# A hybrid transformer block on one core: weights laid out by the host, low halves by accumulating DMA, the residual stream in DRAM, and separate leads for loads and casts

## The chip, the core and the metric

The kernel runs on one core of a Trainium2 chip. The core has a matrix engine (TensorE, PE in the profile, with its weight loads as PEld), three engines for elementwise work (VectorE or DVE, ScalarE or ACT, GpSimd or POOL), and a queue engine (SyncE or SP) that here only issues DMA transfers. Each engine takes its instructions in the order in which the program lists them. The engines share an on-chip memory of 128 partitions (SBUF); matmuls write into eight banks of PSUM. Inputs, weights and the output lie in DRAM.

The metric is the device time of one execution in microseconds (us), lower is better.

## The reference

One layer: an input projection feeds an attention head group and a convolution group, an output projection joins them, and a gated feed-forward network (FFN) follows. Only the last two matter here.

```python
xn = rms_norm(h, norm1_g)
proj = einsum('bsd,dn->bsn', xn, w_in)            # 2048 -> 5120
...                                               # attention and causal convolution
mixed = concatenate([att, u], axis=-1)
h = h + einsum('bsm,md->bsd', mixed, w_out)       # 2048 -> 2048
hn = rms_norm(h, norm2_g)
a  = einsum('bsd,df->bsf', hn, w_gate)            # 2048 -> 5632
bu = einsum('bsd,df->bsf', hn, w_up)              # 2048 -> 5632
h = h + einsum('bsf,fd->bsd', silu(a) * bu, w_down)
```

The sequence has 256 positions, in float32. All weights together are about 200 MB and are read once.

## The kernel before

**Split operands.** PE multiplies operands of a shorter format (fp32r). To keep float32 accuracy every operand is split into a high part (its rounding) and a low part (the rest), and a product is the sum of three matmuls: high × high, high × low, low × high. A weight tile is therefore loaded (`raw`, line 305, by SP), rounded by ACT (`whi`, line 310), and its rest computed by VectorE (`wlo`, line 319: raw − whi). A second way makes the rest without VectorE: ACT writes −whi into `wlo` (line 313), and a POOL DMA adds `raw` to it (line 314). This is "by DMA". The name `by_dma` on a chunk selects it.

**Chunks.** All matrix products form one list of chunks, which `run_chunks` emits in order. A plain chunk is 2 × 128 rows of a weight by 512 columns: 512 KB, 12 matmuls of 512 columns. Chunk t + 2 is loaded and cast ahead of chunk t's multiplication (`AHEAD`); in the fast blocks below loads and roundings run three chunks ahead and subtractions two (`HI_AHEAD`, `LO_AHEAD`). Loads have four `raw` buffers, and every third chunk outside the fast blocks takes a buffer of another pool. `whi` and `wlo` have three each. When a block of columns is complete, a generator (`glu_done`, `out_done`, `block_done`, `down_done`, ...) finishes it, and `resume()` runs the generators step by step between the matmuls.

**Stages.** w_in goes first, in column blocks; then w_out, whose block ends (`out_done`) add the product to the residual stream `h`, kept in SBUF as two tiles of 128 × 2048; then the FFN. Its hidden width of 5632 is eleven blocks of 512 columns, in groups of 4, 4 and 3 (`FGROUPS`). A group computes gate and up for its blocks, transposes the activations, and multiplies them with its rows of w_down; `down_done` adds the result to `h`, and in the last group writes `h` out.

**Fast blocks.** Block 0 uses plain chunks. Blocks 1 to 10 are fast: half of the inner dimension goes through a scheme of seven products for eight. An "s" unit loads two tiles each of w_up and w_gate (`wb`, line 872, two DMAs), forms sums of them on VectorE (`wt`, lines 882 to 884), rounds 7 × 512 columns on ACT (`wh`, lines 885 and 886) and subtracts on VectorE (`wl`, lines 890 and 891); PE then runs 21 matmuls (lines 907 to 909). The other half goes as "g" and "u" units, plain residues of gate and up: a chunk of two tiles, 12 matmuls (lines 924 to 930). A block has four s, four g and four u units in the order of the string `ORDER` (`FIRST` for block 1). The last g and the last u unit of blocks 2 to 10 are by DMA.

At a block's end `products_done` and `block_done` combine eight PSUM sums on VectorE and ACT. `transposed` then turns the activations around on PE (line 801, `ps_a`), in two steps, during the first s unit of the next block; each step's result is split by ACT (`ahi`, line 803) and VectorE (`alo`, line 805).

**Order.** Nothing is scheduled by a machine: each engine's order is the order in which the Python code emits. An instruction that waits holds up all that stand behind it on its engine.

## Time and profile before

| what | value |
|---|---|
| time, median of 3 runs | 1081.56 us (1081.28 to 1082.33) |
| the profiled execution's span | 1078.5 us, granted clock 0.995 |
| matmul instructions of PE | 4834 |
| weights and inputs read | 200.04 MB |
| w_in, w_out | about 6 to 255, 255 to 345 us |
| FFN block 0 | 345 to 397 us |
| fast blocks 1 to 3, their w_down | 397 to 531, 531 to 619 us |
| fast blocks 4 to 7, their w_down | 619 to 789, 789 to 877 us |
| fast blocks 8 to 10, their w_down | 877 to 1004, 1004 to 1074 us |

The profile is of one execution, and its span leaves out what lies around it in the measured time. A row of the timeline gives start and duration in us, the engine, the source line, the operation, what it writes and reads by the program's names (buffer numbers left out), and in brackets how long the engine was idle just before and on which instruction that ended. A matmul's duration is longer than the distance to the next one, since matmuls are pipelined; the distance between starts is the pace.

### The profile page before, as it was taken

Reading aid. Unit: us, or ns where it says so; the run is one execution under the profiler, and the core shown is the slowest. Engines: PE = TensorE matmul, PEld = TensorE weight load, DVE = VectorE, ACT = ScalarE, POOL = GpSimd, SP = SyncE. Lnnn points to the kernel's source line nnn. Section 1 sums busy time; section 2 is a strip of 40 time slices with the busy share of each in tenths; the row PEclk is TensorE's granted clock in tenths of the full one; section 3 lists DMA queues with packets and bytes.
Section 4 is the critical chain, followed back from the end, with each engine's and each line's share of the span. In section 5 each row is a group of like instructions: output and inputs, shape, how many; then the busy total and the mean of one; then the engine's idle time right before and its main releaser. Section 6 shows DMA issues by size and latency. Waiting matters only on the chain.

```text
span 1078.5 us, 13236 instructions
## 1 busy us (share of the span) xinstructions
PE 1054.6 (98%) x4834; PEld 871.6 (81%) x4834; DVE 844.6 (78%) x1025; ACT 587.1 (54%) x765; POOL 62.8 (6%) x101
## 2 busy tenths in 40 slices
PE   8999999999999999899999999999999999999998
PEld 7888888877888887788888888878788888887786
DVE  4799989898765689988754699889865589898553
ACT  6544567755765655555443456655643355555332
POOL 0030021200100000000000000000000000000000
PEclk9999999999999999999999999999999999999999
DMA  8856665554446575576565777767566668666661
GB/s 243 257 178 199 190 185 169 155 173 157 137 156 195 161 248 197 195 215 194 176 215 183 243 248 212 212 214 230 163 201 221 201 215 263 208 207 176 215 210 63
DMA packets 120941, 212.45 MB, mean 197 GB/s; under 512 B 7220, under 2 KB 29166, under 8 KB 120876
## 3 DMA queue, kind: packets, MB, share of 16 engines
q1 hardware_dynamic: 117744, 200.56, 58.2%
q0 software_dynamic: 3072, 11.01, 4.9%
q8 instruction: 38, 0.62, 0.3%
q14 instruction: 27, 0.22, 0.1%
q10 hardware_dynamic: 60, 0.03, 0.0%
HBM read 200.04 MB, written 2.10 MB: 187 GB/s over the span
## 4 chain that ended last, share of the span: by engine, by line
PE 70%; DVE 15%; issue 6%; ACT 5%; DMA 2%; POOL 1%; SPq 0%; DVEq 0%; ACTq 0%
PE acc L355 16%; PE acc L350 16%; PE acc L349 16%; DVE wlo L319 4%; PE q L924 3%; PE q L925 3%; PE q L930 3%; PE q L907 3%; PE q L908 3%; PE q L909 3%; ACT wh L886 3%; DVE wt L882 2%; DVE wt L883 1%; DVE wt L884 1%; DVE y L488 1%
## 5 line engine op out<-in xcount | busy, mean ns | idle before, releaser
L319 DVE TENSOR_TENSOR wlo<-raw,whi 128x1024 fp32r<-128x1024 f32 (+1 forms) x279 | 337.6, 1218 | 136.8 <-ACT whi L310 136.8
L310 ACT CAST whi<-raw 128x1024 fp32r<-128x1024 f32 (+1 forms) x297 | 309.5, 1049 | 226.9 <-PE acc L350 167.0
L350 PE MATMUL acc<-whi,alo 128*128 128x512 f32 x384 | 150.6, 392 | 2.3 <-DVE alo L805 2.3
L349 PE MATMUL acc<-whi,ahi 128*128 128x512 f32 x384 | 150.4, 392 | 0.0
L886 ACT CAST wh<-wt 128x2048 fp32r<-128x2048 f32 x40 | 76.6, 1914 | 128.8 <-DVE wt L884 128.8
L349 PE MATMUL acc<-whi,xhi 128*128 128x512 f32 (+1 forms) x352 | 129.9, 375 | 4.0 <-ACT xhi L224 2.5
L350 PE MATMUL acc<-whi,xlo 128*128 128x512 f32 (+1 forms) x352 | 128.3, 371 | 0.5 <-DVE xlo L225 0.4
L924 PE MATMUL q<-whi,chi 128*128 128x512 f32 x320 | 124.7, 390 | 0.0
L925 PE MATMUL q<-whi,clo 128*128 128x512 f32 x320 | 124.6, 389 | 0.0
L907 PE MATMUL q<-wh,fhi 128*128 128x512 f32 x280 | 111.1, 397 | 2.1 <-DVE alo L805 2.1
L909 PE MATMUL q<-wl,fhi 128*128 128x512 f32 x280 | 110.4, 394 | 2.3 <-DVE wl L891 2.3
L908 PE MATMUL q<-wh,flo 128*128 128x512 f32 x280 | 110.2, 393 | 0.0
L488 DVE SCALAR_TENSOR_TENSOR y<-upad,cw,y 128x256 f32<-128x256 f32 x240 | 103.3, 480 | 2.1 <-ACT y L481 1.6
L355 PE MATMUL acc<-wlo,ahi 128*128 128x512 f32 x384 | 103.7, 391 | 0.0
L891 DVE TENSOR_TENSOR wl<-wt,wh 128x2048 fp32r<-128x2048 f32 x40 | 91.6, 2290 | 9.4 <-ACT wh L886 9.4
L355 PE MATMUL acc<-wlo,xhi 128*128 128x512 f32 (+1 forms) x352 | 88.2, 375 | 1.1 <-DVE wlo L319 1.1
L350 PEld LDWEIGHTS acc<-whi,alo 128*128 128x128 f32 x384 | 72.6, 189 | 17.8 <-DVE alo L805 2.6
L930 PE MATMUL q<-wlo,chi 128*128 128x512 f32 x320 | 86.4, 392 | 0.0
L349 PEld LDWEIGHTS acc<-whi,ahi 128*128 128x128 f32 x384 | 72.5, 189 | 15.3 <-ACT ahi L803 0.2
L355 PEld LDWEIGHTS acc<-wlo,ahi 128*128 128x128 f32 x384 | 71.8, 189 | 14.6
L349 PEld LDWEIGHTS acc<-whi,xhi 128*128 128x128 f32 x352 | 66.3, 188 | 15.9 <-ACT xhi L224 2.9
L350 PEld LDWEIGHTS acc<-whi,xlo 128*128 128x128 f32 x352 | 66.3, 188 | 11.9 <-DVE xlo L225 0.9
(194 smaller groups left out, 1413.5 us busy)
## 6 DMA issues: line engine op xcount, KB each, us to landing
raw<-in_w_down_dram SPq DMA_DIRECT2D x88, 512.0 KB, 4.0
raw<-in_w_in_dram SPq DMA_DIRECT2D x48, 512.0 KB, 3.8
raw<-in_w_gate_dram SPq DMA_DIRECT2D x48, 512.0 KB, 4.6
raw<-in_w_up_dram SPq DMA_DIRECT2D x48, 512.0 KB, 3.8
wb<-in_w_up_dram SPq DMA_DIRECT2D x40, 512.0 KB, 4.4
wb<-in_w_gate_dram SPq DMA_DIRECT2D x40, 512.0 KB, 5.7
raw<-in_w_out_dram SPq DMA_DIRECT2D x32, 512.0 KB, 3.6
raw<-in_w_in_dram SPq DMA_DIRECT2D x62, 256.0 KB, 3.7
```

The costliest lines, as they stand in the source:

```text
L310: act.copy(c["hi"], c["raw"])
L319: dve.tensor_tensor(c["lo"], c["raw"], c["hi"].bitcast(F32), ALU.subtract)
L349: pe.matmul(ps[m], xhi[:, ms], hi[:, j, :], start=c["first"] and j == 0, stop=False)
L350: pe.matmul(ps[m], xlo[:, ms], hi[:, j, :], start=False, stop=False)
L355: pe.matmul(ps[m], xhi[:, ms], lo[:, j, :], start=False, stop=c["last"] and j == nk - 1)
L488: dve.scalar_tensor_tensor(y[:, ct, :], src, wk, y[:, ct, :], ALU.mult, ALU.add)
L907: pe.matmul(ps, fhi[:, f, p, :], c["hi"][:, w], start=bool(first), stop=False)
L908: pe.matmul(ps, flo[:, f, p, :], c["hi"][:, w], start=False, stop=False)
L909: pe.matmul(ps, fhi[:, f, p, :], c["lo"][:, w], start=False, stop=bool(last))
L924: pe.matmul(ps, x1[:, ms], hi[:, i, :], start=i == 0 and bool(c["first"].get(q)), stop=False)
L925: pe.matmul(ps, x2[:, ms], hi[:, i, :], start=False, stop=False)
L930: pe.matmul(sum_bank(c, q), forms["plain"][k][0][:, ms], lo[:, i, :], start=False, stop=i == 1 and bool(c["last"].get(q)))
```

## The change

- **Host-laid weights.** All weights come as one flat array, in which every chunk's bytes stand in the order in which its tile holds them. `weights()` records the pieces while the program is written, and the host fills the array. A chunk is one DMA with 4 KB per partition where before it was pieces of 512 B to 2 KB and, for the paired columns of the convolution blocks, two DMAs; an s unit is one DMA of 1 MB where before it was two.
- **By DMA.** Which units are by DMA is now written in capitals in `ORDER` and `FIRST`: two of four g and three of four u units in blocks 2 to 10 (five of eight; before two of eight), and three in block 1 (before none).
- **h in DRAM.** `out_done` also writes `h` to the output array, by POOL DMAs. The tiles of `h` lie in a pool that ends with the FFN's beginning. In groups 0 and 1 `down_done` no longer adds on VectorE: ACT copies the PSUM sum (`part`), and a POOL DMA adds it into the output array. In the last group SP fetches the array's content (`so_far`, `fetch_sums`), VectorE adds to it, and it is written out as before.
- **Leads and buffers.** In the fast blocks loads run five chunks ahead, ACT's roundings for by-DMA units five, other roundings three, subtractions two. `raw` gets five buffers, `whi` and `wlo` four.

VectorE at the boundary of the fast blocks 5 and 6: the end of one block's sums (lines 987 and 989; 1013 and 1015 in the changed code), then the first s unit of the next and the first `alo`. Before:

```order
L987 TENSOR_TENSOR sum_6121<-q_5870,sum_6121 128x512
L987 TENSOR_TENSOR sum_6123<-q_6042,sum_6123 128x512
L989 TENSOR_TENSOR sum_6121<-sum_6121,sum_6120 128x512
L989 TENSOR_TENSOR sum_6123<-sum_6123,sum_6122 128x512
L319 TENSOR_TENSOR wlo<-raw,whi 128x1024
L882 TENSOR_TENSOR wt<-wb 128x1024
L883 TENSOR_TENSOR wt<-wb,wt 128x512
L884 TENSOR_TENSOR wt<-wt,wb 128x512
L890 TENSOR_TENSOR wl<-wb,wh 128x1536
L891 TENSOR_TENSOR wl<-wt,wh 128x2048
L319 TENSOR_TENSOR wlo<-raw,whi 128x1024
L805 TENSOR_TENSOR alo_6220<-ps_a,ahi_6219 128x512
```

and after:

```order
L1013 TENSOR_TENSOR sum_6115<-q_5865,sum_6115 128x512
L1013 TENSOR_TENSOR sum_6117<-q_6035,sum_6117 128x512
L1015 TENSOR_TENSOR sum_6115<-sum_6115,sum_6114 128x512
L1015 TENSOR_TENSOR sum_6117<-sum_6117,sum_6116 128x512
L907 TENSOR_TENSOR wt<-wb 128x1024
L908 TENSOR_TENSOR wt<-wb,wt 128x512
L909 TENSOR_TENSOR wt<-wt,wb 128x512
L915 TENSOR_TENSOR wl<-wb,wh 128x1536
L916 TENSOR_TENSOR wl<-wt,wh 128x2048
L326 TENSOR_TENSOR wlo<-raw,whi 128x1024
L831 TENSOR_TENSOR alo_6214<-ps_a,ahi_6213 128x512
```

The `wlo` subtraction between the sums and the s unit's `wt` is gone; the one ahead of `alo` stays. (In the changed code the lines stand lower: 310, 313 and 319 are 317, 320 and 326; 803 and 805 are 829 and 831; 882 to 891 are 907 to 916.)

ACT at the same place, from a `wh` to the second `ahi` of the boundary. Before:

```order
L886 CAST wh<-wt 128x2048
L310 CAST whi<-raw 128x1024
L803 CAST ahi_6219<-ps_a 128x512
L310 CAST whi<-raw 128x1024
L313 ACTIVATE wlo<-raw 128x1024
L885 CAST wh<-wb 128x1536
L886 CAST wh<-wt 128x2048
L803 CAST ahi_6269<-ps_a 128x512
```

and after:

```order
L910 CAST wh<-wb 128x1536
L911 CAST wh<-wt 128x2048
L317 CAST whi<-raw 128x1024
L829 CAST ahi_6213<-ps_a 128x512
L317 CAST whi<-raw 128x1024
L320 ACTIVATE wlo<-raw 128x1024
L317 CAST whi<-raw 128x1024
L320 ACTIVATE wlo<-raw 128x1024
L910 CAST wh<-wb 128x1536
L911 CAST wh<-wt 128x2048
L829 CAST ahi_6267<-ps_a 128x512
```

Between the two `ahi` stand two pairs of a rounding and a negated copy where before there was one.

SP at the last w_down, which begins with the w_down rows (`raw`) behind the last unit of block 10. Before:

```order
L872 DMA wb<-in_w_up_dram 128x2x512
L872 DMA wb<-in_w_gate_dram 128x2x512
L305 DMA raw<-in_w_up_dram 128x2x512 x2
L305 DMA raw<-in_w_down_dram 128x2x512 x24
L1004 DMA out_dram<-h_81 128x256 x2
L1004 DMA out_dram<-h_82 128x256 x2
```

and after:

```order
L898 DMA wb<-in_wts_dram 128x2048
L313 DMA raw<-in_wts_dram 128x1024 x9
L1025 DMA so_far<-out_dram 128x512 x2
L313 DMA raw<-in_wts_dram 128x1024 x2
L1025 DMA so_far<-out_dram 128x512 x2
L313 DMA raw<-in_wts_dram 128x1024 x6
L1025 DMA so_far<-out_dram 128x512 x2
L313 DMA raw<-in_wts_dram 128x1024 x6
L1025 DMA so_far<-out_dram 128x512 x2
L313 DMA raw<-in_wts_dram 128x1024 x3
L1044 DMA out_dram<-so_far 128x256 x4
```

The sums' fetches stand among the weight loads now, the first of them behind the loads of the last u units and seven chunks of w_down.

The diff, its core:

```diff
 AHEAD = 2
-RAW_BUFS = 4
+RAW_BUFS = 5
...
 LAG = (3, 2, 6)
-HL_BUFS = 3
+HL_BUFS = 4
...
 TWOS = [tuple(REST[i : i + 2]) for i in range(0, len(REST), 2)]
-BY_DMA = TWOS[-1:]
-
-ORDER = "sggsggsuusuu"
-
-FIRST = "gugusgsusgsu"
+
+ORDER = "sgGsgGsUUsUu"
+
+FIRST = "gugusgsUsGsU"
...
 PRODUCTS = ((Q1, 0, 5), (Q6, 5, 1), (Q7, 6, 2), (Q5, 4, 3), (Q2, 1, 6), (Q4, 3, 0), (Q3, 2, 4))
-HI_AHEAD, LO_AHEAD = 3, 2
+LOAD_AHEAD, DMA_AHEAD, HI_AHEAD, LO_AHEAD = 5, 5, 3, 2
...
     aux_ps = ctx.enter_context(tc.tile_pool(name="aux", bufs=AUX, space=PSUM))
-    h = [const.tile([P, D], F32, tag=f"h{m}", name=f"h{m}") for m in range(NM)]
+    h = [pre.tile([P, D], F32, tag=f"h{m}", name=f"h{m}", bufs=1) for m in range(NM)]
...
                                done=done if i == len(ks) else None, spare=spare, by_dma=False,
-                               rows=slice(part[0], part[-1] + 1), load=load_chunk, round=round_chunk,
+                               load=load_chunk, round=round_chunk,
                                split=split_chunk, multiply=multiply))
+
+    next_weight = [0]
+
+    def weights(parts):
+
+        n = sum(w for _, _, _, w in parts)
+        src = wts[next_weight[0] : next_weight[0] + P * n].rearrange("(p n) -> p n", n=n)
+        placed_at.append((next_weight[0], n, parts))
+        next_weight[0] += P * n
+        return src
...
             c["raw"] = view(wp.tile([P, NK * N], F32, tag="raw", name="raw", bufs=RAW_BUFS))
-        o = 0
-        rows = c["w"].rearrange("(k p) n -> p k n", p=P)
-        for col, n in c["cols"]:
-            sp.dma_start(out=c["raw"][:, :, o : o + n], in_=rows[:, c["rows"], col : col + n])
-            o += n
+        ks = c["ks"] if "ks" in c else range(c["k0"], c["k0"] + c["nk"])
+        src = weights([(c["w"], k, col, n) for k in ks for col, n in c["cols"]])
+        sp.dma_start(out=c["raw"].rearrange("p k n -> p (k n)"), in_=src)
...
         n = len(chunks)
-        i = j = 0
+        loaded = split = 0
+        rounded = [0, 0]
+
+        def load(i):
+            if i in before:
+                before[i]()
+            chunks[i]["load"](chunks[i])
+
+        def do_round(which, until):
+            while rounded[which] < min(n, until):
+                c = chunks[rounded[which]]
+                if c["by_dma"] == bool(which):
+                    c["round"](c)
+                rounded[which] += 1
+
         for t in range(n):
-            hi_lead, lo_lead = lead(t)
-            while j < min(i, t + 1 + lo_lead):
-                chunks[j]["split"](chunks[j])
-                j += 1
-            while i < min(n, t + 1 + hi_lead):
-                if i in before:
-                    before[i]()
-                chunks[i]["load"](chunks[i])
-                chunks[i]["round"](chunks[i])
-                i += 1
-                if hi_lead == lo_lead:
-                    chunks[j]["split"](chunks[j])
-                    j += 1
-            while j < min(n, t + 1 + lo_lead):
-                chunks[j]["split"](chunks[j])
-                j += 1
+            load_lead, dma_lead, hi_lead, lo_lead = lead(t)
+            while split < min(rounded[0], t + 1 + lo_lead):
+                chunks[split]["split"](chunks[split])
+                split += 1
+            while loaded < min(n, t + 1 + load_lead):
+                load(loaded)
+                loaded += 1
+                if load_lead == lo_lead:
+                    do_round(1, loaded)
+                    do_round(0, loaded)
+                    chunks[split]["split"](chunks[split])
+                    split += 1
+            do_round(1, t + 1 + dma_lead)
+            do_round(0, t + 1 + hi_lead)
+            while split < min(n, t + 1 + lo_lead):
+                chunks[split]["split"](chunks[split])
+                split += 1
+            if t in fetch_at:
+                fetch_sums(fetch_at[t])
...
             dve.tensor_tensor(h[m][:, cs], h[m][:, cs], ps[m], ALU.add)
+        for m in range(NM):
+            pool.dma_start(out=out[m * P : (m + 1) * P, cs], in_=h[m][:, cs])
...
         c["b"] = early.tile([P, 4, N], F32, tag="wb", name="wb")
-        for i, w in enumerate((w_up, w_gate)):
-            sp.dma_start(out=c["b"][:, 2 * i : 2 * i + 2, :],
-                         in_=w.rearrange("(k p) n -> p k n", p=P)[:, c["k"] :: HK, c["col"] : c["col"] + N])
+        src = weights([(w, k, c["col"], N) for w in ("w_up", "w_gate") for k in (c["k"], c["k"] + HK)])
+        sp.dma_start(out=c["b"].rearrange("p k n -> p (k n)"), in_=src)
...
         left = dict(s=list(range(NS)), g=list(TWOS), u=list(TWOS))
-        for kind in order:
+        for unit in order:
+            kind = unit.lower()
...
             if kind == "s":
-                c.update(k=what, col=j * N, load=load_pair, round=round_pair, split=split_pair,
+                c.update(k=what, col=j * N, by_dma=False, load=load_pair, round=round_pair, split=split_pair,
...
             else:
-                c.update(ks=what, w=w_gate if kind == "g" else w_up, nk=2, width=N, cols=[(j * N, N)],
-                         rows=slice(what[0], what[1] + 1, what[1] - what[0]), by_dma=j > 1 and what in BY_DMA,
+                c.update(ks=what, w="w_gate" if kind == "g" else "w_up", nk=2, width=N, cols=[(j * N, N)],
+                         by_dma=unit.isupper(),
...
         yield from transposed(j, u)
+    so_far, fetch_at = {}, {}
+
+    def fetch_sums(n):
+        so_far[n] = []
+        for m in range(NM):
+            t = ffn["pool"].tile([P, N], F32, tag=f"sum{n % 2 * NM + m}", name="so_far")
+            sp.dma_start(out=t, in_=out[m * P : (m + 1) * P, n * N : (n + 1) * N])
+            so_far[n].append(t)
+
...
         cs = slice(n * N, (n + 1) * N)
-        parts = 2 if g == len(FGROUPS) - 1 and n == D // N - 1 else 1
-        for m in range(NM):
+        if g < len(FGROUPS) - 1:
+            for m in range(NM):
+                t = ffn["pool"].tile([P, N], F32, tag=f"sum{n % 2 * NM + m}", name="part")
+                act.copy(t, ps[m])
+                pool.dma_start(out=out[m * P : (m + 1) * P, cs], in_=t, accum_op=ALU.add)
+            return
+        parts = 2 if n == D // N - 1 else 1
+        for m in range(NM):
+            t = so_far[n][m]
...
                 hs = slice(cs.start + i * w, cs.start + (i + 1) * w)
-                dve.tensor_tensor(h[m][:, hs], h[m][:, hs], ps[m][:, ws], ALU.add)
-                if g == len(FGROUPS) - 1:
-
-                    (sp if n == D // N - 1 else pool).dma_start(out=out[m * P : (m + 1) * P, hs], in_=h[m][:, hs])
+                dve.tensor_tensor(t[:, ws], t[:, ws], ps[m][:, ws], ALU.add)
+                (sp if n == D // N - 1 else pool).dma_start(out=out[m * P : (m + 1) * P, hs], in_=t[:, ws])
...
             at = len(chunks)
-            block(w_down, n * N, range(j0 * 4, (j0 + nb) * 4), fa, lambda ps, g=g, n=n: down_done(g, n, ps))
+            if g == len(FGROUPS) - 1:
+                fetch_at[at + (0 if n else FGROUPS[g] * N // P // NK - 2)] = n
+            block("w_down", n * N, range(j0 * 4, (j0 + nb) * 4), fa, lambda ps, g=g, n=n: down_done(g, n, ps))
...
         j0 += nb
-    lead = lambda t: (1, 1) if t < len(XPARTS) else (HI_AHEAD, LO_AHEAD) if "kind" in chunks[t] else (AHEAD, AHEAD)
+    lead = lambda t: ((1,) * 4 if t < len(XPARTS) else (LOAD_AHEAD, DMA_AHEAD, HI_AHEAD, LO_AHEAD)
+                      if "kind" in chunks[t] else (AHEAD,) * 4)
...
     run_chunks()
-_FLAT = {"x": (S, D), "w_in": (D, 5120), "conv_w": (1, W, 1, CC), "w_out": (D, D), "w_gate": (D, FF),
-         "w_up": (D, FF), "w_down": (FF, D)}
+_FLAT = {"x": (S, D), "conv_w": (1, W, 1, CC)}
+_WEIGHTS = {"w_in": (D, 5120), "w_out": (D, D), "w_gate": (D, FF), "w_up": (D, FF), "w_down": (FF, D)}
...
     given["rope"] = rope_constants()
+    total = sum(a * b for a, b in _WEIGHTS.values())
+    flat = np.empty(total, np.float32)
+    given["wts"] = flat
...
     args.append(nc.dram_tensor("out_0_dram", (S, D), F32, kind="ExternalOutput").ap())
+    placed_at = []
     with tile.TileContext(nc) as tc, tc.manual_schedule():
-        tile_block(tc, *args)
+        tile_block(tc, *args, placed_at)
+    ws = {name: np.asarray(inputs[name], dtype=np.float32).reshape(shape) for name, shape in _WEIGHTS.items()}
+    assert sum(P * n for _, n, _ in placed_at) == total
+    for o, n, parts in placed_at:
+        tiles = [ws[w][k * P : (k + 1) * P, col : col + c] for w, k, col, c in parts]
+        flat[o : o + P * n] = np.concatenate(tiles, axis=1).ravel()
```

More of the change, by code (lines that the diff above doesn't have):

```diff
@@ L104, in tile_block @@
     tc: tile.TileContext,
-    x, w_in, conv_w, w_out, w_gate, w_up, w_down, gains, vecs, rope, out,
+    x, conv_w, gains, vecs, rope, wts, out, placed_at,
 ):
@@ L1012, in tile_block @@
     for nct in CONV_BLOCKS:
-        block(w_in, [(GC + c0 * P, nct * P), (AC + c0 * P, nct * P)], range(KD), fx,
+        block("w_in", [(GC + c0 * P, nct * P), (AC + c0 * P, nct * P)], range(KD), fx,
               lambda ps, c0=c0, nct=nct: glu_done(c0, nct, ps), cuts=[len(p) for p in XPARTS] if c0 == 0 else ())
@@ L1016, in tile_block @@
     for b in range(2):
-        block(w_in, KC + b * N, range(KD), fx, lambda ps, b=b: qk_done("k", b, ps))
-        block(w_in, QC + b * N, range(KD), fx, lambda ps, b=b: qk_done("q", b, ps))
+        block("w_in", KC + b * N, range(KD), fx, lambda ps, b=b: qk_done("k", b, ps))
+        block("w_in", QC + b * N, range(KD), fx, lambda ps, b=b: qk_done("q", b, ps))
     for b in range(2):
-        block(w_in, VC + b * N, range(KD), fx, lambda ps, b=b: v_done(b, ps))
+        block("w_in", VC + b * N, range(KD), fx, lambda ps, b=b: v_done(b, ps))
     for ks, first, last in ((range(0, 4), True, False), (range(4, 8), False, False), (range(8, 16), False, True)):
         for n in range(3):
-            block(w_out, n * N, ks, fm, (lambda ps, n=n: out_done(n, ps)) if last else None,
+            block("w_out", n * N, ks, fm, (lambda ps, n=n: out_done(n, ps)) if last else None,
                   bkey=("o", n), first=first, last=last, spare=n == 2)
-    block(w_out, 3 * N, range(16), fm, lambda ps: out_done(3, ps))
+    block("w_out", 3 * N, range(16), fm, lambda ps: out_done(3, ps))
     for i, c in enumerate(chunks[len(XPARTS) : -12]):
```

4 lines of the change are left out of this document (2 added, 2 removed).

## The prediction

> **What bounds the kernel now.** I read the page first, then the clock by core, the table by stage, TensorE's waits, and the timelines around the longest of them.
>
> ```profile
> PE 1054.6 (98%) x4834; PEld 871.6 (81%) x4834; DVE 844.6 (78%) x1025; ACT 587.1 (54%) x765; POOL 62.8 (6%) x101
> core 0: 1078.5 us, clock 0.995
> 397.00:455.00 58.00, 55.59 (x242) 44.85 (x240) 55.66 (x53) 31.05 (x27) 0.00 (x0) 0.97 0.62 211
> 455.00:498.00 43.00, 40.59 (x175) 33.40 (x176) 39.24 (x39) 24.85 (x23) 1.99 (x2) 0.96 0.73 219
> 667.00:711.00 44.00, 44.00 (x201) 36.37 (x200) 40.23 (x39) 25.77 (x24) 1.77 (x2) 1.00 0.72 215
> 1004.00:1030.00 26.00, 23.69 (x102) 19.14 (x101) 17.43 (x21) 9.81 (x12) 1.14 (x2) 0.93 0.51 172
> PE ps_a L801 <- DVE alo L805: 5.1, 5, 1.2
> ```
>
> The window rows give start and end, length, busy time of PE, PEld, DVE, ACT and POOL, the granted clock, the DMA share and GB/s. PE is busy 98% of the span and the change leaves its list of matmuls as it is, so only PE's stalls can be won. The windows are the first fast gate-and-up block (397), the second (455), a later one (667) and the start of the last w_down (1004). VectorE works 55.66 of 58 us in the first and 40.23 of 44 us in the later one: there it is all but full, and PE's stalls follow it. Start, duration and instruction are the columns below:
>
> ```profile
> 410.32 0.39 PE L909 MATMUL q<-wl,fhi 128*128 128x512 f32 x1
> 412.82 0.50 PE L907 MATMUL q<-wh,fhi 128*128 128x512 f32 x1 [2.11 <-DVE alo L805]
> ...
> 414.45 0.63 PE L909 MATMUL q<-wl,fhi 128*128 128x512 f32 x1
> 414.88 0.63 PE L907 MATMUL q<-wh,fhi 128*128 128x512 f32 x1
> ...
> 454.30 0.40 PE L908 MATMUL q<-wh,flo 128*128 128x512 f32 x1
> 456.18 0.50 PE L909 MATMUL q<-wl,fhi 128*128 128x512 f32 x1 [1.48 <-DVE wl L891]
> 457.92 1.05 PE L801 MATMUL ps_a<-ident,sum 128*128 128x128 f32 x4 [1.23 <-DVE alo L805]
> ...
> 713.40 0.39 PE L907 MATMUL q<-wh,fhi 128*128 128x512 f32 x1
> 713.63 0.39 PE L908 MATMUL q<-wh,flo 128*128 128x512 f32 x1
> 714.30 0.51 PE L909 MATMUL q<-wl,fhi 128*128 128x512 f32 x1 [0.29 <-DVE wl L891]
> 716.04 0.66 PE L801 MATMUL ps_a<-ident,sum 128*128 128x128 f32 x4 [1.23 <-DVE alo L805]
> 757.42 0.39 PE L908 MATMUL q<-wh,flo 128*128 128x512 f32 x1
> ...
> 1018.52 0.40 PE L349 MATMUL acc<-whi,ahi 128*128 128x512 f32 x1
> 1021.23 0.80 PE L350 MATMUL acc<-whi,alo 128*128 128x512 f32 x1 [2.31 <-DVE alo L805]
> ```
>
> Undisturbed matmuls follow each other at 713.63 − 713.40 = 0.23 us (0.227 over longer runs). What a stall costs is the step between starts less that pace:
> - First and second fast block: 412.82 − 410.32 − 0.23 = 2.27; 457.92 − 454.30 − 0.46 = 3.16. After both, the pace falls to 414.88 − 414.45 = 0.43. The clock columns price this: 0.03 × 58 + 0.04 × 43 = 3.4 us. Sum C = 8.8.
> - Later boundaries: 716.04 − 713.63 − 0.45 = 1.96. Of the five waits of transposes for `alo` (5.1 us), four like the two shown make 4.9, so the fifth is 0.2; one of the four is that at 457.92, which leaves three boundaries of this kind. Sum D = 5.9.
> - Start of the last w_down: 1021.23 − 1018.52 − 0.23 = 2.48, and 0.07 × 26 = 1.8 of clock. Sum E = 4.3.
>
> **Accumulating DMAs for VectorE's subtractions.** The same boundary on VectorE, the last one's two rows, and the costs by group:
>
> ```profile
> 706.18 1.22 DVE L319 TENSOR_TENSOR wlo<-raw,whi 128x1024 fp32r<-128x1024 f32 x1
> ...
> 711.96 2.29 DVE L891 TENSOR_TENSOR wl<-wt,wh 128x2048 fp32r<-128x2048 f32 x1 [0.31 <-ACT wh L886]
> 714.17 1.22 DVE L319 TENSOR_TENSOR wlo<-raw,whi 128x1024 fp32r<-128x1024 f32 x1
> 715.30 0.68 DVE L805 TENSOR_TENSOR alo<-ps_a,ahi 128x512 fp32r<-128x512 f32 x1
> ...
> 715.16 1.46 ACT L885 CAST wh<-wb 128x1536 fp32r<-128x1536 f32 x1
> 718.61 1.91 ACT L886 CAST wh<-wt 128x2048 fp32r<-128x2048 f32 x1 [1.99 <-DVE wt L884]
> ...
> 1018.27 1.05 ACT L310 CAST whi<-raw 128x1024 fp32r<-128x1024 f32 x1
> 1019.35 1.23 DVE L319 TENSOR_TENSOR wlo<-raw,whi 128x1024 fp32r<-128x1024 f32 x1 [2.41 <-ACT whi L310]
> ...
> L313 ACT ACTIVATE wlo<-raw 128x1024 fp32r<-128x1024 f32 x18 | 19.1, 1059 | 0.0
> L314 POOL DMA_DIRECT2D wlo<-raw x18 | 16.1, 894 | 613.8 <-DVE wlo L319 227.5 <-DVE wl L891 215.4 <-ACT wlo L313 134.2
> q1 hardware_dynamic: 117744, 200.56, 58.2%
> q0 software_dynamic: 3072, 11.01, 4.9%
> wlo<-raw POOLq DMA_DIRECT2D x18, 512.0 KB, 6.9
> ```
>
> By-DMA residues go from 18 to 48: two to five in nine blocks, none to three in the first fast block. VectorE loses 30 subtractions of 1.22 us: 3.66 of its 40.23 us in a later block. One of them, at 706.18, stood ahead of the s unit's whole chain (wt, wh on ACT, wl), two more earlier in the block. The late wl (0.29) needs 0.5 us and the late `alo` 1.5 us, so 3.66 us of room covers both unless ACT ends later. D falls by 5.4, between 0 (ACT decides instead) and 5.9.
>
> ACT gains 30 negated copies of 1.06 us, three in a block: 25.77 + 3.2 = 29 us of 42, not full. But they come five units ahead, so the second `ahi` of a boundary stands behind whi, wlo, whi, wlo, wh, wh rather than whi, wlo, wh, wh. From the end of the first `ahi` that is 2 × (1.05 + 1.06) + 1.46 + 1.91 = 7.6 us, where before it was 5.5 and a wait of 1.99 for VectorE: 0.1 later, if the wait goes. Two of a block's casts must also wait until PE frees one of the four whi buffers, and hold up what ACT has behind them. I put +1 in all, from 0 to +4.5 (0.5 us at nine boundaries, a quarter of one cast pair's 2.1).
>
> POOL issues three more DMAs a block, 0.89 us each, with a median landing 6.9 us later; the residue is used five units of 2.7 to 4.8 us after its cast, at least 13 us. Nothing waits there, by this estimate.
>
> In the first fast block three subtractions go, and the loads' lead of five replaces what this row shows just ahead of it:
>
> ```profile
> 394.81 1.05 ACT L310 CAST whi<-raw 128x1024 fp32r<-128x1024 f32 x1 [3.55 <-DMA raw<-in_w_up_dram]
> ```
>
> ACT was idle 3.55 us for a load, and VectorE behind it. I leave 0.9 of the stall of 2.27 and 0.3 of the second one, and take the slow pace after both as gone: C falls by 7.6, between 4.7 (half of the stalls and of the slow pace stay) and 8.5.
>
> **The last w_down.** `alo` stood behind a `wlo` that waited 2.41 us for a cast issued behind `ahi` on ACT. The changed order puts that cast ahead of `ahi`; only the 0.68 us `alo` remains, and 0.3 of E stays: −4.0, between 0 and −4.3.
>
> **h in DRAM.** Sixteen additions leave VectorE; sixteen ACT copies and accumulating DMAs replace them in the w_down of groups 0 and 1, where PE does not stall for ACT now: nothing, and the cover is the two chunks of 2.7 us each that stand ready while ACT copies. The eight writes of h lie beside the last w_out. In the last w_down SP fetches the sums; the first fetch waits on SP for the output's last accumulation and holds back weight loads behind it. I put +0.5, between 0 and +2.7 (one chunk of 12 matmuls at 0.227).
>
> **Weights laid out by the host.** Same bytes, one DMA for two in the first columns.
>
> ```profile
> PE acc L349 <- ACT xhi L224: 2.5, 2, 1.5
> PE acc L349 <- ACT whi L310: 1.5, 2, 0.8
> raw<-in_w_in_dram SPq DMA_DIRECT2D x48, 512.0 KB, 3.8
> raw<-in_w_in_dram SPq DMA_DIRECT2D x62, 256.0 KB, 3.7
> 3.61 0.95 SPq L305 DMA_DIRECT2D raw<-in_w_in_dram  x2
> ```
>
> A pair cost SP 0.95 us, one costs half; three pairs stand ahead of the fourth x load. PE waited 4.0 us in all at the start. I take half, −2; between 0 and −4. Later on I cost the layout at nothing, since the lead hides a landing: of one matrix, 256 KB took 3.7 us to land and 512 KB 3.8, so longer transfers are no dearer here. That cover would go only with (b) below.
>
> **Sum.** −7.6 − 5.4 − 4.0 − 2.0 + 1.0 + 0.5 = −17.5. The profiled execution has a span of 1078.5; the median of the runs shown, 1081.56, is 3.1 more, which I keep. 1061.0 + 3.1 = 1064.
>
> **Rivals.** (a) *ACT takes VectorE's place.* For it: wh and `ahi` are already VectorE's only wait in the rows above, and ACT now carries four casts between them. If each of nine boundaries keeps or regains 1.1 us, 10 of the 17.5 come back: 1074. Against it: 29 of 42 us.
>
> (b) *The DMA engines become the bound*, the slower end. Loads: 58.2% of 1078.5 for 200.56 MB is 3.13 us per MB; accumulations: 4.9% for 11.01 MB is 4.80. A block loads 2 matrices of 2048 × 512 floats, 8.39 MB, 26.3 us, and accumulates 0.524 MB per residue, 2.5 us; with two that is 31.3 us (0.72 × 44 = 31.7 in the row), with five 38.9. A block lasts 757.42 − 713.63 = 43.8 us, without its stall 41.8: an occupancy of 93%. If the mixture runs 15% slower than these prices, 44.7 us, eight blocks lose 2.9 each (the first is covered by the lead): 1064 + 23 = 1087. At 13% slower, 44.0 a block, the whole gain is spent. For it: no window of before is above 0.73, so this load has not been seen; against it: it is still under 1, loads stand five units ahead, so that their mean rate counts and not one landing, and larger transfers did not land later.
> [...]
>
> (c) *The slow pace is not the stalls' doing.* If it stays when the stalls shrink, 3.4 + 1.8 = 5.2 us of the gain do not come: 1069. Against it, the pace drops right behind the stall at 410.32, and no such stretch lies in the windows with clock 1.00.
> [...]
>
> (d) *Little is won*: stalls move to other places and the time ends between 1078 and 1086.
>
> **How the numbers follow.** Forecast 0.50, with a range of its own of 1058 to 1069; (a) 0.20; (b) 0.13; (c) 0.08; (d) 0.09, of which 0.05 within 0.2% (about 2.2 us, what a measurement of this kernel can tell from no change) and 0.04 slower. Faster 0.50 + 0.20 + 0.08 = 0.78, slower 0.13 + 0.04 = 0.17. The predicted time is the likeliest, 1064. The range goes from 1058, where the start and the first block give their bounds, to 1079, past (a), and leaves out (b) and most of (d).
>
> **What the profile would show.** Right: no PE wait above 0.5 us for wl or `alo` at the later boundaries, a clock of 1.00 in the second fast block, DVE near 36 us and ACT near 29 of a later block of about 42 us, a DMA share near 0.9, and PE's two start waits at about half. Wrong by (a): PE waits for `alo` while VectorE waits for ACT `ahi` or wh. By (b): waits for raw or wb, loads landing far later than after 3.8 us, and residues that PE waits for. By (c): clock 0.96 without a stall ahead of it. At SP's fetch: PE waiting for whi behind raw in the last w_down.

## The result: slower

| | time, median | ratio to before |
|---|---|---|
| before | 1081.42 us | |
| after | 1119.76 us (1114.74 to 1126.2) | 1.0365 (1.0339 to 1.0391) |

The forecast was 1064 us, faster. The page of the changed kernel:

```profile
span 1112.9 us, 13204 instructions
PE 1062.0 (95%) x4834; PEld 876.7 (79%) x4834; DVE 801.9 (72%) x979; ACT 617.8 (56%) x811; POOL 112.3 (10%) x155
```

VectorE works 43 us less than before, as the change meant, and the span is 34.4 us longer. The execution that the profile shows took 1114.74 us, the shortest of the four, so the stages below add up to 34.4 us of loss where the medians differ by 38.3. Stage by stage, from the first matmul of a stage to the first of the next, for the last one to its last matmul (read from PE's timeline, in us; the names of the other kernels are those of the experiments below):

| kernel | blocks 1 to 3 | blocks 4 to 7 | blocks 8 to 10 | last w_down |
|---|---|---|---|---|
| before | 134.8 | 170.1 | 126.4 | 70.2 |
| after | 128.0 | 191.9 | 141.5 | 74.5 |
| ring4x | 129.3 | 171.0 | 127.6 | 75.4 |
| two_of_eight | 133.7 | 171.3 | 127.3 | 75.7 |
| share_alone | 142.4 | 190.8 | 141.9 | 70.3 |
| ring4x_pool_fetch | 131.8 | 170.0 | 127.2 | 70.1 |
| ring4x_pool_fetch_lead3 | 129.3 | 168.8 | 124.9 | 68.6 |
| alo_ahead | 129.0 | 168.2 | 125.2 | 66.8 |

The first three fast blocks gained 6.8 us, about as forecast. Blocks 4 to 7 lost 21.8, blocks 8 to 10 15.1, the last w_down 4.3; the sum is 34.4. The rest stayed: the w_down of groups 0 and 1 take 88.0 us in both kernels, so the ACT copies and DMAs that replace VectorE's additions there cost nothing in those stages.

What PE waited for in the changed kernel (us in total, times, longest):

```profile
PE q L955 <- DMA wlo<-raw: 29.8, 7, 7.1
PE acc L357 <- DVE alo L831: 6.7, 1, 6.7
PE acc L356 <- ACT xhi L223: 3.2, 2, 2.4
PE ps_a L827 <- DVE alo L831: 0.9, 1, 0.9
PE acc L356 <- ACT whi L317: 0.7, 1, 0.7
```

The old waits of transposes for `alo` are down from 5.1 to 0.9 us. A new wait stands in their place, for the low halves that the accumulating DMAs make. Its first case, on PE:

```profile
621.73 0.39 PE L950 MATMUL q<-whi,clo 128*128 128x512 f32 x1
629.27 2.08 PE L955 MATMUL q<-wlo,chi 128*128 128x512 f32 x4 [7.15 <-DMA wlo<-raw]
```

And POOL's queue around it:

```profile
618.45 0.87 POOL L1034 DMA_DIRECT2D out_dram<-part  x1 [4.19 <-issue]
622.36 0.87 POOL L321 DMA_DIRECT2D wlo<-raw  x1 [3.04 <-ACT whi L317]
629.53 0.89 POOL L321 DMA_DIRECT2D wlo<-raw  x1 [6.30 <-issue]
636.97 0.87 POOL L321 DMA_DIRECT2D wlo<-raw  x1 [6.56 <-issue]
```

"issue" means that POOL waited for no instruction that the profile shows. The DMA of 622.36 landed 6.9 us after its issue, at 629.2, and PE went on at 629.27; the next one was issued at 629.53. Each accumulating DMA of these blocks begins 0.31 us after the one ahead of it has landed. All twenty of blocks 4 to 7 together:

```profile
L321 POOL DMA_DIRECT2D wlo<-raw x20: 862/872/885, 622.4 to 791.9; - x20
  issue: 88.7, 11
DMA to landing us min/median/max: 5.6/8.5/11.2
```

(791.9 − 622.4) / 19 = 8.92 us for each, five of them 44.6 us, in a block of 42: the queue is full, and PE ends up waiting for it. For the others of the twenty the list names ACT or VectorE; those too were issued 0.31 us after the landing ahead of them. In the kernel before, POOL's DMAs of these blocks stand far apart:

```profile
649.09 0.90 POOL L314 DMA_DIRECT2D wlo<-raw  x1 [18.33 <-DVE wt L882]
671.90 0.88 POOL L314 DMA_DIRECT2D wlo<-raw  x1 [21.91 <-DVE wlo L319]
```

The table by stage (columns as in the prediction) shows the rest:

```profile
397.00:452.00 55.00, 53.89 (x243) 43.97 (x241) 52.17 (x48) 37.29 (x34) 4.41 (x5) 1.00 0.87 278
452.00:494.00 42.00, 41.08 (x186) 34.09 (x186) 36.84 (x36) 28.32 (x28) 4.32 (x5) 1.00 0.88 263
612.60:660.00 47.40, 34.30 (x139) 27.60 (x138) 27.46 (x21) 28.13 (x25) 6.09 (x7) 0.89 0.74 191
1034.00:1060.00 26.00, 19.34 (x82) 15.56 (x81) 10.90 (x13) 7.59 (x9) 0.00 (x0) 0.87 0.46 164
```

Block 2 (the second row) is as the prediction had it: 36.84 us of VectorE and 28.32 of ACT in 42 us, a DMA share of 0.88, a clock of 1.00. The DMA share is lower, not higher, where PE waits: 0.74 and 0.46 in the last two rows, against 0.87 and 0.88.

### The profile page after: what moved, and what is told of

It reads as the page before. It is cut to its first block, busy times and chain, and to the rows that moved or that the text cites. A ratio compares the mean times of both kernels' runs of the same rounds, so it can differ in the third digit from the quotient of the medians.

```text
span 1112.9 us, 13204 instructions
## 1 busy us (share of the span) xinstructions
PE 1062.0 (95%) x4834; PEld 876.7 (79%) x4834; DVE 801.9 (72%) x979; ACT 617.8 (56%) x811; POOL 112.3 (10%) x155
## 4 chain that ended last, share of the span: by engine, by line
issue 28%; PE 25%; DMA 9%; DVE 3%; ACT 1%; POOL 1%; POOLq 0%; SPq 0%; DVEq 0%; ACTq 0%
PE acc L357 5%; PE acc L356 5%; PE acc L362 5%; DMA wlo<-raw 5%; DMA raw<-in_wts_dram 4%; PE q L955 2%; PE q L950 1%; PE q L949 1%; PE q L932 1%; PE q L933 1%; PE q L934 1%; POOL out_dram L1034 1%; ACT wh L911 1%; POOL wlo L321 0%; DVE wlo L326 0%
## 5 line engine op out<-in xcount | busy, mean ns | idle before, releaser
L317 ACT CAST whi<-raw 128x1024 fp32r<-128x1024 f32 (+1 forms) x297 | 305.7, 1049 | 188.5 <-PE acc L357 96.7
L326 DVE TENSOR_TENSOR wlo<-raw,whi 128x1024 fp32r<-128x1024 f32 (+1 forms) x249 | 299.9, 1220 | 143.2 <-ACT whi L317 142.9
L949 PE MATMUL q<-whi,chi 128*128 128x512 f32 x320 | 124.9, 390 | 0.0
L955 PE MATMUL q<-wlo,chi 128*128 128x512 f32 x320 | 91.3, 409 | 29.8 <-DMA wlo<-raw 29.8
L911 ACT CAST wh<-wt 128x2048 fp32r<-128x2048 f32 x40 | 76.4, 1911 | 44.6 <-DVE wt L909 44.0
L915 DVE TENSOR_TENSOR wl<-wb,wh 128x1536 fp32r<-128x1536 f32 x40 | 70.1, 1754 | 42.3 <-ACT wh L910 42.3
L955 PEld LDWEIGHTS q<-wlo,chi 128*128 128x128 f32 x320 | 60.7, 195 | 45.4 <-DMA wlo<-raw 33.7
```

The source lines that it names most:

```text
L317: act.copy(c["hi"], c["raw"])
L326: dve.tensor_tensor(c["lo"], c["raw"], c["hi"].bitcast(F32), ALU.subtract)
L949: pe.matmul(ps, x1[:, ms], hi[:, i, :], start=i == 0 and bool(c["first"].get(q)), stop=False)
L955: pe.matmul(sum_bank(c, q), forms["plain"][k][0][:, ms], lo[:, i, :], start=False, stop=i == 1 and bool(c["last"].get(q)))
```

## Experiments

The theory after the two profiles (S): POOL's DMA queue takes one accumulating DMA at a time. The profile shows no instruction that POOL waits for there; what the kernel does set is `dynamic_dma_scratch_size`, 512 in both kernels. The theory takes that for the size of the room in which the queue keeps its DMAs, and calls it the descriptor store; that is the author's estimate, and ring4x and ring2x change nothing but this number. Rivals: the DMA engines are crowded (B, the prediction's slower end), or the new leads or the layout cost the time (L). For the last w_down, theory F: the fetch on SP.

**ring4x: a larger descriptor store**

```diff
-    nc = _bacc.Bacc("TRN2", ..., dynamic_dma_scratch_size=512)
+    nc = _bacc.Bacc("TRN2", ..., dynamic_dma_scratch_size=2048)
```

> The changed kernel with the descriptor store of POOL's DMA queue four times as large (2048 bytes per partition instead of 512); nothing else differs. Theory S (one at a time): with the small store POOL can't issue an accumulating DMA before the one ahead of it has landed (in the changed kernel each is issued 0.31 us after the previous landing, and POOL waits for no instruction there), so five a block at 8.4 us and 0.3 us fill 43.6 us of a block of 42. Then, with the larger store, DMAs are issued 0.9 us after ACT's copy, PE's 29.8 us of waits for wlo go to under 5 us, blocks 4 to 7 take 168 to 172 us instead of 191.6, and the time falls from 1119.8 to between 1078 and 1090 (the wait of 6.7 us in the last w_down stays). Theory B (bandwidth): the DMA engines are the limit; then issues come earlier but landings grow to 13 us and more, PE still waits over 20 us for wlo, and the time stays above 1105.

Measured: 1081.84 us, ratio 1.0014 (0.9999 to 1.0028). Blocks 4 to 7 take 171.0 us. The twenty accumulating DMAs of blocks 4 to 7:

```profile
L321 POOL DMA_DIRECT2D wlo<-raw x20: 854/862/880, 616.7 to 763.2; - x20
  ACT wlo L320: 109.3, 16
DMA to landing us min/median/max: 4.5/7.2/11.7
```

No "issue" is left: POOL now waits for ACT's negated copy, and issues. What PE and VectorE wait for, in the two fences below:

```profile
PE acc L357 <- DVE alo L831: 6.7, 1, 6.7
PE ps_a L827 <- DVE alo L831: 5.7, 6, 1.2
PE q L955 <- DMA wlo<-raw: 0.3, 1, 0.3
```

```profile
DVE wl L915 <- ACT wh L910: 28.8, 10, 4.7
```

The same bytes move at the same places, and 38 us are back. S holds, and B falls: landings did not grow to 13 us (median 7.2, longest 11.7 in these blocks), though up to four are under way at once, the last sums of w_down included. The first three blocks keep 5.5 us of their gain, and the last w_down is 5.2 us longer than before. In blocks 4 to 10 none of the forecast gain is there: VectorE idles 28.8 us for `wh`, and the transposes wait 5.7 us for `alo` again.

**ring2x: twice the store**, 1024 for 512, otherwise as above.

> The changed kernel with the descriptor store twice as large (1024 bytes per partition). Theory S: it holds the descriptors of two or three accumulating DMAs, so a DMA is issued while the one ahead is still under way, and only the DMA after those waits for a landing; five a block are then 22 to 30 of 42 us, PE waits less than 2 us for wlo, and the time is within 4 us of the 1081.8 with four times the store. If the store isn't what POOL waits for, each is still issued 0.31 us after the landing of the one ahead, and the time is above 1105.

Measured: 1080.89 us, 1.0009 (0.9993 to 1.0025).

```profile
L321 POOL DMA_DIRECT2D wlo<-raw x20: 857/870/887, 617.6 to 762.8; - x20
  ACT wlo L320: 107.8, 16
DMA to landing us min/median/max: 4.5/6.9/12.5
```

Twice the store suffices: PE waits for no accumulating DMA. In these blocks two residues at most are under way at a time, three DMAs with the sums of w_down. At the start of block 8 a fourth has to wait: two sums and a residue are under way, ACT's copy for the next residue is ready at 876.79, and POOL issues it at 878.29, 0.30 us after the first sum has landed.

**two_of_eight: the old share, all else changed**

```diff
-ORDER = "sgGsgGsUUsUu"
-FIRST = "gugusgsUsGsU"
+ORDER = "sggsgGsuusuU"
+FIRST = "gugusgsusgsu"
```

> The changed kernel with the share of the kernel before: the last gate and the last up residue of blocks 2 to 10 by DMA, none in block 1; layout, leads, buffers and h in DRAM stay changed. Both theories S and B expect no wait of PE for wlo by DMA and blocks 4 to 7 back at about 168 to 171 us. If the rest of the change is harmless but for the last w_down, 1075 to 1088; if it is the leads or the layout that cost time (theory L), blocks 4 to 7 stay above 180 us and the time above 1100.

Measured: 1089.06 us, 1.0086 (1.0071 to 1.0101), a little above the expected band. PE's two largest waits:

```profile
PE ps_a L827 <- DVE alo L831: 7.9, 7, 1.2
PE acc L357 <- DVE alo L831: 7.0, 1, 7.0
```

No wait for a DMA is left, so the share is needed for the loss. The rest of the change is not neutral: it costs 8 us, of which the last w_down has 5.5; blocks 4 to 10 are 2.1 longer, with seven waits of transposes for `alo` where there were five of 5.1 us.

**share_alone: the new share on the kernel before**

```diff
-ORDER = "sggsggsuusuu"
-FIRST = "gugusgsusgsu"
+ORDER = "sgGsgGsUUsUu"
+FIRST = "gugusgsUsGsU"
...
-        for kind in order:
+        for unit in order:
+            kind = unit.lower()
...
-   by_dma=j > 1 and what in BY_DMA,
+   by_dma=unit.isupper(),
```

> The kernel before with the share alone: the same five of eight residues (three of block 1) by accumulating DMA, with its own leads of three and two, its own buffers, loads and h in SBUF. Theory S: POOL's queue is full here too, and the shorter lead leaves less slack, so PE waits for wlo in blocks 2 to 10, 20 us or more in all, and the time is 1100 to 1130. Theory L (the new leads or the layout cost the time): no such waits, and 1065 to 1082.

Measured: 1127.14 us, 1.0444 (1.0422 to 1.0465).

```profile
PE q L930 <- DMA wlo<-raw: 37.6, 19, 4.3
```

The share alone makes the loss; L is not needed. That it is in more and shorter waits than in the changed kernel goes with the shorter lead, which no run separates. The share with a larger store on the kernel before was not tried.

**four_of_eight: one residue less, small store**

```diff
-ORDER = "sgGsgGsUUsUu"
+ORDER = "sgGsgGsUusUu"
```

> The changed kernel with its small descriptor store, but four of eight residues by DMA in blocks 2 to 10 (one up residue less). Theory S: four DMAs of 8.7 us, one at a time, are 35 of a block's 42 us; the queue catches up, PE's waits for wlo by DMA go from 29.8 to under 4 us, and the time falls from 1119.8 to 1080 to 1092, although the store is as small as before. If any crowding of the DMA engines rather than a full queue were the cause, a fifth fewer additions would leave at least half of the waits: above 1098.

Measured: 1097.58 us, 1.0154 (1.0136 to 1.0173).

```profile
PE q L955 <- DMA wlo<-raw: 14.5, 2, 8.1
```

A miss on the size, by 6 us. By their size alone the waits, half of the 29.8 us, don't tell a full queue from crowded DMA engines; their places do. The two stand at the first residue by DMA of blocks 4 and 8; in the other blocks there is none, so four a block do fit one at a time. What I had left out is how a group begins: the last two sums of w_down are accumulating DMAs in the same queue, and the first residues stand behind them. The same holds for the changed kernel: its first residue of block 4 is issued 9.7 us after the block's first matmul, with the store of ring4x 3.1 us after it, and the waits at the first residues of blocks 4 and 8 are 7.15 and 5.88 of its 29.8 us.

**fetch_on_pool: the sums fetched by POOL**

```diff
-            sp.dma_start(out=t, in_=out[m * P : (m + 1) * P, n * N : (n + 1) * N])
+            pool.dma_start(out=t, in_=out[m * P : (m + 1) * P, n * N : (n + 1) * N])
```

> The changed kernel with the fetches of the sums in the last w_down issued by POOL instead of SP. Theory F: the fetch on SP waits for the sum tiles that the last transposes free, holds back the load of a w_down chunk (issued at 1048.09), and through it the cast, the subtraction and the alo behind it on VectorE; then the wait of 6.66 us for alo in the last w_down falls below 1 us and this stage (74.5 us) takes 67 to 69. By the rival, that alo waits for its own transposes or for VectorE's work, it stays above 5 us. Blocks 4 to 10 stay as they are: 1109 to 1115 in all, with a spread like that of the changed kernel.

In the changed kernel SP, ACT and VectorE stand like this at that place (start, duration; SP's rows are issues, with the time that they held the queue):

```profile
1035.72 12.32 SPq L1025 DMA_DIRECT2D so_far<-out_dram  x2
1048.09 0.90 SPq L313 DMA_DIRECT2D raw<-in_wts_dram  x2
```

```profile
1047.82 0.59 ACT L829 CAST ahi<-ps_a 128x512 fp32r<-128x512 f32 x1 [3.45 <-PE ps_a L827]
1052.66 1.04 ACT L317 CAST whi<-raw 128x1024 fp32r<-128x1024 f32 x1 [4.25 <-DMA raw<-in_wts_dram]
```

```profile
1053.74 1.23 DVE L326 TENSOR_TENSOR wlo<-raw,whi 128x1024 fp32r<-128x1024 f32 x1 [7.32 <-ACT whi L317]
1054.88 0.68 DVE L831 TENSOR_TENSOR alo<-ps_a,ahi 128x512 fp32r<-128x512 f32 x1
```

Measured with the fetch on POOL: 1115.85 us, 1.0333 (1.0317 to 1.035); the last w_down 70.3 us, not 67 to 69. PE's waits:

```profile
PE q L955 <- DMA wlo<-raw: 32.8, 8, 7.7
PE acc L357 <- DVE alo L831: 2.3, 1, 2.3
```

F is right in its mechanism: with SP free, 4.4 us of the wait go. (11.7 of the 12.32 us on SP were a wait for PE's transposes, which read the sum tiles.) But not to below 1 us: 2.3 are left, the same as before the change. The stall that the change was to remove is still there behind the one that it added, and for the old reason: the cast that the subtraction ahead of `alo` needs stands behind `ahi` on ACT, here (`ahi` at 1051.21, casts from 1051.70) as before the change (1017.79 and 1018.27).

**ring4x_pool_fetch: both**

> The changed kernel with both: the descriptor store four times as large, and the fetches of the sums issued by POOL. Theories S and F, which the runs before bear out one by one: the gains add up, since they lie in different stages. From the 1081.8 of the larger store the stall at the start of the last w_down falls from 6.85 to 2.48 us, as it did with the small store: 1081.8 - 4.4 = 1077.4, and up to 1.5 less for the slow pace behind it; 1075 to 1079, 0.2 to 0.5% faster than before. By the rival, that the two share something (POOL's queue is then fuller at the end), 1080 to 1083.

Measured: 1076.83 us, 0.9962 (0.9946 to 0.9977). The two gains add up; VectorE's wait for `wh` stays, and ACT waits for loads (the profiled execution is the longest of the seven, 1080.51 us):

```profile
DVE wl L915 <- ACT wh L910: 32.1, 11, 4.7
ACT whi L317 <- DMA raw<-in_wts_dram: 39.1, 12, 6.1
```

**ring4x_pool_fetch_lead3: and the roundings for DMA three units ahead**

```diff
-LOAD_AHEAD, DMA_AHEAD, HI_AHEAD, LO_AHEAD = 5, 5, 3, 2
+LOAD_AHEAD, DMA_AHEAD, HI_AHEAD, LO_AHEAD = 5, 3, 3, 2
```

> The same, with ACT's roundings for residues by DMA three units ahead (as the other roundings are) instead of five. Theory A: with five, such a rounding waits on ACT for a load that lands late and holds up the wh behind it; VectorE then idles (28.8 us in ten waits for wh), its sums at the block's end come late, and alo makes the transposes wait (5.7 us in six waits). Then VectorE's waits for wh fall below 10 us, the transposes' waits below 2, and the time is 3 to 5 us lower than with five: 1072 to 1075. Rival: with three units of lead (8 to 14 us, less the queue on ACT) a landing of 7 to 13 us comes too late, PE waits for wlo 10 us or more in all, and the time is above 1082.

Measured: 1073.36 us, 0.9929 (0.9914 to 0.9944). The same two waits, and PE's for the DMAs:

```profile
DVE wl L915 <- ACT wh L910: 6.0, 4, 2.8
ACT whi L317 <- DMA raw<-in_wts_dram: 9.5, 6, 4.1
```

```profile
PE q L955 <- DMA wlo<-raw: 3.4, 5, 1.4
```

Theory A holds: the lead of five put casts on ACT ahead of `wh` that had to wait for their loads. With three, ACT's wait for loads goes from 39.1 to 9.5 us and VectorE's from 32.1 to 6.0, no transpose waits for `alo` at a boundary, and 3.5 us are gained; 3.4 us of waits for the DMAs are the price.

**alo_ahead: alo one step earlier in the last block**

```diff
-            yield from lag(2)
+            yield from lag(1 if j == FF // N - 1 else 2)
             dve.tensor_tensor(lo, pt, hi.bitcast(F32), ALU.subtract)
```

> The kernel with the larger store, fetches by POOL and a lead of three, and one thing more: alo of the last block's transposes is issued one step earlier, so that on VectorE it stands ahead of a w_down subtraction instead of behind it. Theory E: the stall of 2.49 us at the start of the last w_down is alo behind that wlo, which waits for ACT's whi (2.97 us of VectorE's time); ahi is ready before. Then PE waits under 0.6 us there, the slow pace behind it (clock 0.93 over 26 us before) goes too, and the time falls from 1073.4 by 2 to 4: 1069 to 1071.5. Rival: alo waits for ahi itself, which comes as late; then the stall stays above 2 us and the time within 1 us of 1073.4.

Measured: 1069.01 us, 0.9885 (0.9872 to 0.9899), the fastest of all. The same window as the prediction's fourth, first in the run before this one and then here (the last w_down begins at 997.11 and at 996.38), and PE's wait and VectorE's rows here:

```profile
1004.00:1030.00 26.00, 23.69 (x109) 19.28 (x108) 13.15 (x13) 10.35 (x12) 2.75 (x5) 1.00 0.68 246
```

```profile
1004.00:1030.00 26.00, 25.50 (x116) 20.79 (x114) 13.24 (x13) 11.29 (x12) 2.75 (x5) 1.00 0.71 254
```

```profile
PE acc L357 <- DVE alo L831: 0.5, 1, 0.5
```

```profile
1009.96 1.23 DVE L326 TENSOR_TENSOR wlo<-raw,whi 128x1024 fp32r<-128x1024 f32 x1 [2.89 <-ACT whi L317]
1011.10 0.68 DVE L831 TENSOR_TENSOR alo<-ps_a,ahi 128x512 fp32r<-128x512 f32 x1
```

The stall is down to 0.5 us. The last w_down takes 66.8 us, 1.8 less than in the run before this one and 3.4 less than in the kernel before, of the 4.0 that the prediction put on this place. The medians fall by 4.35 us; where the rest of that lies, the two traces don't show, since the clock of this window was 1.00 in both, with the stall of 2.3 us and without it. And the mechanism holds in part only: the `alo` that PE waits for still stands behind a subtraction that waits 2.89 us for a cast. It comes earlier because its transposes do: its `ahi` ends 12.6 us after the stage's first matmul, in the run before this one 14.4.

**layout_alone: host-laid weights on the kernel before**

```diff
-        for col, n in c["cols"]:
-            sp.dma_start(out=c["raw"][:, :, o : o + n], in_=rows[:, c["rows"], col : col + n])
+        src = weights([(c["w"], k, col, n) for k in ks for col, n in c["cols"]])
+        sp.dma_start(out=c["raw"].rearrange("p k n -> p (k n)"), in_=src)
```

> The kernel before with nothing but the weights laid out by the host: one DMA of 4 KB per partition for a chunk, one of 8 KB for an s unit. The prediction's term for the layout: PE's start waits fall from 4.0 us to about 2, and the rest stays: 1079 us. Rival: the first x loads, which land after 5.8 us before and 7.8 us in the changed kernel, share the DMA engines with larger weight transfers and come no earlier, so the waits for xhi stay and the time is within 0.2% of before.

Measured: 1081.02 us, 0.9996 (0.9987 to 1.0005). PE's start waits and the DMA rows of this kernel, and then one DMA row of the kernel before:

```profile
PE acc L357 <- ACT xhi L224: 3.1, 2, 2.6
PE acc L357 <- ACT whi L318: 0.7, 1, 0.7
```

```profile
q1 hardware_dynamic: 51168, 200.56, 54.8%
h<-in_x_dram SPq DMA_DIRECT2D x6, 256.0 KB, 7.7
```

```profile
h<-in_x_dram SPq DMA_DIRECT2D x6, 256.0 KB, 5.8
```

The rival is right: the layout is worth nothing here. The transfers do take less of the DMA engines (54.8% of the span rather than 58.2%, for the same bytes), but those of x, each issued at the same time or earlier, land 7.7 us after their issue instead of 5.8, and the wait has only moved from `whi` to `xhi`.

## Why the prediction was wrong

- **The step that failed** is one sentence in the part on accumulating DMAs: POOL issues three more, each lands a median of 6.9 us later, "Nothing waits there, by this estimate." It took landings as independent of one another. With this store they are not: the queue handles one at a time, at 8.92 us each, so five need 44.6 us of a block of 42. The profile of before could not show that, since it has two a block, some 20 us apart, and none behind another. It did show a median landing of 6.9 us, and multiplying it by five (35 us of 42) would have shown how little room a queue without overlap has; that bound was missing from the range. The part on `h` in DRAM priced its accumulating DMAs at nothing; the last two of each w_down stand in the same queue, ahead of the first residues of blocks 4 and 8.
- **Rival (b)** had the slower end, but not for this reason: the DMA engines are busy at 0.88 and finish the same work in time when the store is larger. That the additions and loads add up in one DMA share is right (0.88 is near the 0.93 worked out), and landings were longer beside loads: in ring4x 4.5 us with a DMA share of 0.61 during the landing, 13.05 with a share of 1.0. But sharing alone cost PE 0.3 us in ring4x. The mixture did not run 13% slower than the prices that the prediction took, but a little faster: in block 2 of the changed kernel 0.88 of 42 us are 37.0, and the prices gave 38.9.
- **C** (−7.6): −6.8 measured, stall and slow pace. As steps less the pace, the first stall is 1.27 rather than 0.9 and the second 1.08 rather than 0.3, and no slow pace is left (clock 1.00 in blocks 1 and 2).
- **D** (−5.4): the mechanism is right, the size depends on ACT. With the queue full, the late residues hid it; with the queue mended (ring4x), the stages gained nothing, since **rival (a)** held: ACT's casts stood ahead of `wh`. Its place was not the boundary's two `ahi`, as I had it, but earlier in the block, where a cast waits for its load (37.8 us of ACT's time in ring4x), not for a `whi` buffer. With a lead of three, blocks 4 to 10 gain 2.8 us over before.
- **E** (−4.0): +4.3 in the changed kernel. The prediction said that the changed order puts the cast ahead of `ahi`. It does not: the rows under fetch_on_pool have `ahi` at 1047.82 and the cast at 1052.66, and `alo` still stood behind that cast's subtraction. The cast waited besides for a load, which SP's fetch held back. I had priced the fetch at +0.5, up to +2.7 for one chunk; it cost 4.4 us of waiting, since the whole chain from load to `alo` hangs on it.
- **Start** (−2): nothing, as layout_alone shows.
- **Rival (c)**: fell as it was put. Where the stalls shrank to 1.3 us and less, the clock is 1.00 in blocks 1 and 2; the slow pace went with them. But a stall does not bring it by its length alone: the same step of 2.48 us that the prediction priced with 1.8 us of slow pace had none behind it in ring4x_pool_fetch_lead3. The last section has the counts.

In all, the stalls that the prediction counted were the right ones. What the loss adds up to: the seven steps of PE at the late residues are 30.9 us longer than its pace; the two stages lost 36.9 although 5.9 of old stalls went, so about 12 us, by difference, are slow pace behind the new stalls. The clock records agree in the main: 21.3 us of these stages run at half the clock behind the waits, a loss of 10.7.

Not tried: `h` in DRAM alone. Its parts are known only by the stages (w_down of groups 0 and 1 unchanged, the last one with the fetch).

## What to carry to other kernels

When work moves to a queue, price the queue as well as the transfer: how long one takes times how many there are, against the period, as if none overlapped and with everything that shares the queue, until a trace shows that they do (here 5 × 8.92 us in a block of 42). An idle time that ends with "issue", 0.31 us behind the landing of the transfer ahead, was the mark of a full queue here; look for a setting of the queue's size before giving the transfers less to do: 1024 for 512 brought back 38.9 us here, one residue less a block 22.2. And an instruction that is issued early on an engine that works in order takes its wait along: a cast five units ahead held up work that was due at once (VectorE's waits for `wh` were 32.1 us with a lead of five, 6.0 with three).

## What the hardware showed that I had not expected

- What POOL's DMAs did changed with `dynamic_dma_scratch_size` alone. With 512 there was one accumulating DMA at a time, of 128 × 4 KB or of 128 × 2 KB, each that stood ready issued 0.31 us after the landing ahead of it; with 1024 up to three were under way, with 2048 up to four, at median landings of 6.9 and 7.2 us in blocks 4 to 7. Two plain POOL DMAs of 128 × 2 KB did overlap with 512 (issued at 1060.58 and 1061.22, landed at 1063.78 and 1064.33 in the changed kernel). That this size is the limit is shown by changing it alone (1119.76 us with 512, 1080.89 with 1024, 1081.84 with 2048); what it is the size of, and how much of it one such DMA takes, no run shows.
- PE's slow pace came in stretches of 3.41 us, or several of them, at half the clock, and all stretches of one execution began on one grid of 3.41 us (in the kernel before at 413.67, 458.04 and 1021.24, 13 and then 165 steps apart; in the changed kernel at 625.44, 656.16, 792.69, 905.33, 932.64 and 1052.10, whole steps apart too). Counted over the twelve traces from 20 us on: where PE ran at the full clock and was idle for 2.05 us or more of a grid step, the next step was at half the clock, 33 times of 33; where it was idle for 1.0 to 1.83 us, once of 50 times. (The kernel before and the changed one have nine of the former, of 2.06 to 3.41 us, and six of the latter, of 1.11 to 1.54 us; a slow step followed each of the nine and none of the six.) In these traces, then, it mattered where a stall lay: the 2.31 us in the kernel before lay within one step, the 2.31 us in ring4x_pool_fetch_lead3 lay across two, with 1.21 and 1.10 us, and the clock stayed at 1.00.
- Weight pieces of 4 and 8 KB instead of 512 B to 2 KB lowered the DMA engines' time for the same 200.56 MB from 58.2% of 1078.5 us to 54.8% of 1079.4, 6%, and the kernel's time not at all.
